# Transposed input requested from ScalarE's queue, warm-up on a cleared buffer, last square sum on VectorE

## The chip, the cores and the metric

The kernel runs on one core of a Trainium2 chip. Its time is the device time of one execution, in microseconds (us); three executions of the kernel before took 984.0, 983.96 and 982.06 us, with a median of 983.96. One more execution was recorded by the hardware profiler, and all rows below come from that one.

## The reference

Two layers of a hybrid decoder act on x, 256 positions of 2048 features. Each layer normalises x, multiplies it by one wide input matrix, feeds three causal mixers from the result (a convolution, a gated delta rule, a dilated attention), and adds the gated mixer outputs through one output matrix:

```
for l in range(2):
    h = x * rsqrt(mean(x*x) + eps) * norm_w[l]
    u = h @ w_in[l]                          # 2048 x 7692
    y = [conv(u) | gated_deltanet(u) | dilated_attention(u)], each times silu(gate)
    x = x + y @ w_out[l]                     # 2048 x 2048
out = x * rsqrt(mean(x*x) + eps) * final_norm_w
```

## The kernel before, in words

Every large product is made from three partial products: a float32 operand is split into a high part, rounded by ScalarE (`split_hi`, or the first line of `split`), and the rest, made by VectorE (`split_lo`, or its second line). TensorE adds high x high, high x low and low x high into a PSUM tile `acc`. The tiles HT_71 and HT_72 hold high and low part of the normalised input, whi and wlo those of a weight piece.

For layer 0 the input is read a second time in a layout by channel, x_t: 16 blocks of 128 channels x 256 positions. `load_xt` reads one or two blocks into a buffer b_0 to b_8 and `norm_xt` splits them with the layer's weight column from the parameter tile par; so block k of HT needs an x_t transfer, one ScalarE and one VectorE instruction. The row scale rsqrt(mean(x*x)) is applied later to the products; its square sums come from x itself, read in eight pieces by `load_x`, squared and added up on ScalarE.

Weights arrive in pieces (`load_weights`), in four raw buffers, requested by SyncE's queue (SP). A raw buffer is free again when VectorE has made its wlo. `project` walks over the jobs. The first job has 396 columns: for each of the 16 channel blocks one `unit` of six products (two row tiles, three parts each). The sixteen units take nine weight pieces: two of one block, seven of two blocks.

The order of the instructions on each engine is not that of the code. The class `Plan` runs all the generators as tasks, gives each instruction an assumed duration, and appends next the one that could start first in that reckoning. What it assumes decides the order; the engines then work through their lists strictly as written, with semaphores between them. A DMA takes one of eight semaphores in turn (DMAHW0 to DMAHW7), and a request waits at its engine until the DMA that had the same semaphore before has landed.

At the end, the last job makes its two row tiles one after the other (`last_unit`). For each, `last_residual` adds the residual, sums the squares of the last 256 columns, finishes the row scale on VectorE and GpSimd, multiplies by the final weight, scales and writes out.

Of the kernel before, what the change touches and what calls it, by code (L numbers as in the profile page):

```python
# [11 lines left out]
F32 = mybir.dt.float32  # L12
F32R = mybir.dt.float32r
BF16 = mybir.dt.bfloat16
AF = mybir.ActivationFunctionType
ALU = mybir.AluOpType
# [5 lines left out]
S = 256  # L22
DEPTH = 2
# [141 lines left out]
def _free(ap):  # L165
    n = 1
    for s in ap.shape[1:]:
        n *= s
    return n
# [3 lines left out]
def hybrid_trunk(ctx, tc, x, x_t, w_in, conf_pw_w, w_out, params, final_norm_w, rope, lnc, out):  # L173
    nc = tc.nc
    cp = ctx.enter_context(tc.tile_pool(name="consts", bufs=1))
    wp = ctx.enter_context(tc.tile_pool(name="weights", bufs=1))
    sp = ctx.enter_context(tc.tile_pool(name="work", bufs=1))
# [3 lines left out]
    plan = Plan()  # L181


    def act(out_, in_, func=AF.Copy, scale=1.0, bias=0.0, accum=None):
        n_ap = sum(not isinstance(v, (int, float)) for v in (scale, bias)) + (accum is not None)
        kw = {} if accum is None else {"accum_out": accum}
        return ("act", 95 + _free(out_) / 1.2 + 93 * n_ap,
                lambda: nc.scalar.activation(out_, in_, func, bias=bias, scale=scale, **kw))  # L188
# [6 lines left out]
    def tt(out_, a, b, op):  # L195
        return ("dve", 70 + _free(out_) / 0.96, lambda: nc.vector.tensor_tensor(out_, a, b, op=op))  # L196

    def ts(out_, a, s1, s2, op0, op1=None):
        extra = 60 if not isinstance(s1, (int, float)) else 0

        def emit():
            if op1 is None:
                nc.vector.tensor_scalar(out_, a, s1, None, op0=op0)  # L203
            else:
                nc.vector.tensor_scalar(out_, a, s1, s2, op0=op0, op1=op1)
        return ("dve", 70 + _free(out_) / 0.96 + extra, emit)
# [32 lines left out]
    def summax(out_, a, b, mx):  # L239

        return ("dve", 130 + _free(out_) / 0.96, lambda: nc.vector.tensor_tensor_reduce(
            out=out_, in0=a, in1=b, scale=1.0, scalar=-3.0e38, op0=ALU.add, op1=ALU.max, accum_out=mx))

    def gpow(out_, a, e):
        return ("pool", 350 + 165 * _free(out_), lambda: nc.gpsimd.tensor_tensor(out_, a, e, op=ALU.pow))  # L245

# [18 lines left out]
    JUNK = sp.tile([128, 512], BF16, name="JUNK")  # L265
# [7 lines left out]
    def small(shape, name):  # L273
# [4 lines left out]

    xf = x.rearrange("b s d -> (b s) d")
    of = out.rearrange("b s d -> (b s) d")  # L280
    ident = cp.tile([128, 128], F32, name="ident")
    make_identity(nc, ident)
    ones = cp.tile([128, 128], F32, name="ones")
# [6 lines left out]
    PAR = [cp.tile([128, PCOLS], F32, name=f"par{l}") for l in range(DEPTH)]  # L290
# [2 lines left out]
    PIECES, LAST_PIECES = W_OUT_BLOCKS  # L293
    GROUPS = [(0, 768), (768, 768), (1536, 512)]
    X_PIECES = [(256 * i, 256) for i in range(8)]
    XT_BEFORE = {0: (0, 1), 1: (1, 1), **{i: (2 * i - 2, 2) for i in range(2, 9)}}
    X_BEFORE = {8 + j: j for j in range(len(X_PIECES))}
    SSQ = [cp.tile([128, NT, len(p)], F32, name=f"ssq{l}")
           for l, p in enumerate([X_PIECES] + [PIECES] * (DEPTH - 1) + [LAST_PIECES])]
# [8 lines left out]
    def warm_up(n):  # L308

        ps = yield ("get", MIX)  # L310
        yield ("pe", 107.0, lambda: [nc.tensor.transpose(ps[:, :128], ones, ident) for _ in range(n)])
        yield ("put", MIX, [ps])

    def setup_consts():
# [10 lines left out]
    def setup(l):  # L325

        if l:
            yield ("wait", conv_ready[0])
        yield ("dma", 200.0 if l else 0.0, lambda: (nc.sync if l else nc.scalar).dma_start(PAR[l], params[l]))
        yield ("set", misc_ready[l])  # L330
        yield act(AEXP[l], PAR[l][:, P_AL:P_AL + H], AF.Exp)
        yield ts(PAR[l][:, P_DW:P_DW + 4 * CW], PAR[l][:, P_DW:P_DW + 4 * CW], 0.5, None, ALU.mult)
        yield ts(GNH[l], PAR[l][:, P_GN:P_GN + 1], 0.5, None, ALU.mult)
        yield ("set", conv_ready[l])

    def split(hi, lo, src, scale):

        yield act(hi, src, scale=scale)
        yield stt(lo, src, scale, hi.bitcast(F32), ALU.mult, ALU.subtract)
# [19 lines left out]
    def load_xt(k0, m):  # L359

        buf = yield ("get", S768)
        yield ("dma", 128 * m * S * 4 / 330.0, lambda: nc.sync.dma_start(  # L362
            buf[:, :m * S], bass.AP(tensor=x_t.tensor, offset=x_t.offset + k0 * S, ap=[[KB * S, 128], [1, m * S]])))
        plan.spawn(norm_xt(k0, m, buf), 2)

    def norm_xt(k0, m, buf):
        yield ("wait", misc_ready[0])
        for b in range(m):
            k = k0 + b
            yield from split(HT[0][:, k, :], HT[1][:, k, :], buf[:, b * S:(b + 1) * S], PAR[0][:, k:k + 1])  # L370
            yield ("set", h_ready[0][k])
        yield ("put", S768, [buf])

    def load_x(j):

        c0, n = X_PIECES[j]
        buf = yield ("get", S768)
        xs = buf[:, :NT * n].rearrange("p (t c) -> p t c", t=NT)
        yield ("dma", 128 * NT * n * 4 / 330.0, lambda: nc.sync.dma_start(
            xs, xf[:, c0:c0 + n].rearrange("(t p) c -> p t c", p=128)))  # L380
        plan.spawn(sums_x(j, xs, buf), 3)
        if j == len(X_PIECES) - 1:
            nc.sync.dma_start(lncs, lnc)
            nc.sync.dma_start(ropes, rope.rearrange("(t p) c -> p t c", p=128))
# [5 lines left out]
    def load_weights(order):  # L390
        for i in order:
            src, m, n, _ = chunks[i]
            if i in XT_BEFORE:
                yield from load_xt(*XT_BEFORE[i])
            if i in X_BEFORE:
                yield from load_x(X_BEFORE[i])
            raw = yield ("get", RAW)
            view = raw[:, :m * n].rearrange("p (a n) -> p a n", n=n)
            flat_ = raw[:, :m * n]
            if m > 2:  # L400
                flat_ = flat_.rearrange("p (a n) -> p a n", n=2 * n)
            raw_ready[i][1] = (raw, view)
            yield ("dma", 128 * m * n * 4 / 330.0,
                   lambda src=src, flat_=flat_: nc.sync.dma_start(flat_, src))  # L404
            yield ("set", raw_ready[i][0])
# [158 lines left out]
    def layer(l):  # L564
# [612 lines left out]
        def last_residual(j):  # L1177

            c0, n = pieces[j]
            end = j == len(pieces) - 1  # L1180

            def then(acc, tile_=None):
                yield ("wait", xs_ready[j // 2])
                if j == 0:
                    plan.spawn(load_final(), 30)
                for t in range(NT) if tile_ is None else [tile_]:
                    xv = xs[j][t]
                    yield tt(xv, acc[t][:, :n], xv, ALU.add)
                    yield act(JUNK[:, :n], xv, AF.Square, accum=SSQ[DEPTH][:, t, j:j + 1])
                    if end:  # L1190
                        plan.spawn(finish_norm(DEPTH, [], t, t + 1), 1)
                    elif j == len(pieces) - 2:
                        m = sums[:, t:t + 1]
                        yield ("dve", 90.0, lambda: nc.vector.tensor_reduce(m, SSQ[DEPTH][:, t, :j + 1], AX.X, ALU.add))
                        yield ts(m, m, 1.0 / D, 1e-6, ALU.mult, ALU.add)
                    yield ("wait", fw_ready)
                    yield tt(xv, xv, FW[j], ALU.mult)
                    if end:
                        plan.spawn(final(t), 2)
                if not end:  # L1200
                    yield ("put", ACC, [acc])
            return then

        def load_final():
            bufs = yield ("get", S768, 3)
            for j, (c0, n) in enumerate(LAST_PIECES):
                FW[j] = bufs[j // 2][:, (j % 2) * 384:(j % 2) * 384 + n]
                nc.gpsimd.dma_start(FW[j], bass.AP(tensor=final_norm_w.tensor, offset=final_norm_w.offset + c0,
                                                   ap=[[0, 128], [1, n]]))
            yield ("pool", 8000.0, lambda: None)  # L1210
            yield ("set", fw_ready)

        def final(t):
            yield ("wait", final_ready[t])
            r = RSTD[DEPTH][:, t:t + 1]
            for g, eng in ((2, "dve"), (0, "act"), (1, "dve")):
                c0, n = GROUPS[g]
                xv = xg[g][t]
                dma = nc.scalar if eng == "act" else nc.sync
                yield act(xv, xv, scale=r) if eng == "act" else ts(xv, xv, r, None, ALU.mult)  # L1220
                dma.dma_start(of[t * 128:(t + 1) * 128, c0:c0 + n], xv)
                plan.now.end = 0.0
# [31 lines left out]
        return jobs, bg  # L1254

    setup_consts()
    plan.spawn(warm_up(10), 0)
    plan.spawn(warm_up(5), 0, 5000.0)
    for l in range(DEPTH):
        plan.spawn(setup(l), 40 if l else -2)  # L1260
    plan.spawn(finish_norm(0, nsq0), 3)
# [69 lines left out]
```

## Time and profile before

| what | value |
|---|---|
| median of three runs | 983.96 us (982.06 to 984.0) |
| profiled execution | 982.4 us |
| its span, first to last instruction | 980.7 us |
| TensorE busy | 968.4 us, 99% |
| VectorE busy | 749.3 us, 76% |
| ScalarE busy | 550.8 us, 56% |

The profiled execution is 1.7 us longer than its span, and 1.56 us under the median of the runs. TensorE is busy from 12.7 us to 972.4 us almost without a gap; what is not TensorE lies in the first 13 us and the last 8 us.

### The profile page before, as it was taken

To read this page: it belongs to the slowest core of one execution; us is meant where nothing else is said; L and a number is where in the kernel's file an instruction comes from. 1 tells how busy PE (TensorE), PEld (TensorE's weight loads), DVE (VectorE), ACT (ScalarE), POOL (GpSimd) and SP (SyncE) were. 2 spreads that over 40 slices of the span, in tenths; PEclk is the share of its full clock that TensorE was granted. 3 is DMA by queue.
4 is the path that set the end of the run, shared out by engine and by line. 5 is a ranking of instruction groups with operands and counts; after the bars stand their busy time and mean duration, and the time that the engine had idled before them with its cause. 6 is when DMAs were issued, how large, how long until landed. Compare 5 with 4: busy or idle time off the path is not lost.

```text
span 980.7 us, 19060 instructions
## 1 busy us (share of the span) xinstructions
PE 968.4 (99%) x7259; PEld 946.3 (96%) x7259; DVE 749.3 (76%) x1519; ACT 550.8 (56%) x1079; POOL 48.5 (5%) x70
## 2 busy tenths in 40 slices
PE   8999999999999999999999999999999999999996
PEld 7999999999999999999899999999899999999996
DVE  7687799999999666655558768999999976666672
ACT  7764355446685764554455633554466767544551
POOL 1002100200010000000000020002000100000000
PEclk9999999999999999999999999999999999999998
DMA  9765565644445535776655545556344556366672
GB/s 328 254 195 169 175 191 180 186 146 145 146 138 174 178 113 181 224 239 219 214 190 193 192 161 175 186 180 188 128 147 140 155 182 200 127 192 213 220 248 87
DMA packets 67037, 179.01 MB, mean 183 GB/s; under 512 B 8000, under 2 KB 12224, under 8 KB 66944
## 3 DMA queue, kind: packets, MB, share of 16 engines
q1 hardware_dynamic: 64880, 173.85, 54.7%
q0 software_dynamic: 1632, 3.02, 1.2%
q8 instruction: 57, 0.93, 0.4%
q10 hardware_dynamic: 432, 0.91, 0.3%
q14 instruction: 36, 0.29, 0.1%
HBM read 172.77 MB, written 4.98 MB: 181 GB/s over the span
## 4 chain that ended last, share of the span: by engine, by line
PE 97%; DVE 1%; DMA 1%; issue 1%; SPq 0%; ACT 0%; POOLq 0%; POOL 0%; DVEq 0%; ACTq 0%
PE acc L448 87%; PE mix L229 6%; PE mix L236 3%; DMA b<-in_x_t 1%; PE acc L457 1%; PE mix L747 0%; DVE wlo L196 0%; DVE b L193 0%; SPq L404 0%; SPq L362 0%; DVE inv L209 0%; ACT whi L188 0%; POOLq L1327 0%; POOL rstd L245 0%; DVE PTs L203 0%
## 5 line engine op out<-in xcount | busy, mean ns | idle before, releaser
L188 ACT ACTIVATE whi<-raw 128x768 fp32r<-128x768 f32 (+4 forms) x389 | 339.7, 873 | 361.4 <-PE acc L448 320.6
L196 DVE TENSOR_TENSOR wlo<-raw,whi 128x768 fp32r<-128x768 f32 (+4 forms) x389 | 385.5, 991 | 186.4 <-ACT whi L188 182.7
L448 PE MATMUL acc<-HT,whi 128*128 128x256 f32 x2304 | 411.0, 280 | 0.0
L448 PEld LDWEIGHTS acc<-HT,whi 128*128 128x128 f32 x2304 | 351.6, 188 | 1.5 <-issue 1.5
L448 PE MATMUL acc<-HT,wlo 128*128 128x256 f32 x1152 | 321.4, 279 | 0.0
L448 PE MATMUL acc<-whi,HT 128*128 128x384 f32 (+1 forms) x1024 | 271.1, 346 | 0.7 <-ACT whi L188 0.6
L448 PEld LDWEIGHTS acc<-HT,wlo 128*128 128x128 f32 x1152 | 216.0, 188 | 0.0
L448 PEld LDWEIGHTS acc<-whi,HT 128*128 128x128 f32 x1024 | 180.1, 189 | 3.3 <-ACT whi L188 1.4
L448 PE MATMUL acc<-wlo,HT 128*128 128x384 f32 (+1 forms) x512 | 172.9, 338 | 0.8 <-DVE wlo L196 0.8
L448 PE MATMUL acc<-whi,YT 128*128 128x384 f32 (+2 forms) x640 | 163.0, 338 | 0.0
L193 DVE SCALAR_TENSOR_TENSOR b<-b,par,b 128x255 f32<-128x255 f32 (+20 forms) x348 | 153.6, 465 | 0.3
L448 PEld LDWEIGHTS acc<-whi,YT 128*128 128x128 f32 x640 | 114.3, 187 | 2.8
L448 PE MATMUL acc<-wlo,YT 128*128 128x384 f32 (+2 forms) x320 | 107.9, 337 | 0.0
L448 PEld LDWEIGHTS acc<-wlo,HT 128*128 128x128 f32 x512 | 96.2, 188 | 1.8 <-DVE wlo L196 1.8
L448 PEld LDWEIGHTS acc<-wlo,YT 128*128 128x128 f32 x320 | 60.1, 188 | 1.5
L188 ACT ACTIVATE b<-mix 128x384 f32<-128x384 f32 (+3 forms) x96 | 39.6, 425 | 20.1 <-PE mix L229 12.6
L229 PE MATMUL mix<-b,b 128*128 128x128 f32 (+5 forms) x456 | 46.0, 285 | 0.0
L236 PE MATMUL mix<-ident,b 128*128 128x128 f32 x280 | 45.7, 274 | 0.0
L229 PEld LDWEIGHTS mix<-b,b 128*128 128x128 f32 (+3 forms) x456 | 36.2, 161 | 6.7 <-issue 2.2
L236 PEld LDWEIGHTS mix<-ident,b 128*128 128x128 f32 x280 | 34.2, 140 | 3.7 <-issue 1.3
L193 DVE SCALAR_TENSOR_TENSOR b<-b,b 128x256 f32<-128x256 f32 (+3 forms) x62 | 31.5, 511 | 2.6 <-ACT b L188 2.5
L188 ACT ACTIVATE b<-b,stat 128x128 f32<-128x128 f32 (+1 forms) x68 | 29.1, 442 | 6.0 <-DVE stat L203 5.9
(146 smaller groups left out, 613.2 us busy)
## 6 DMA issues: line engine op xcount, KB each, us to landing
raw<-in_w_in SPq DMA_DIRECT2D x240, 384.0 KB, 3.0
raw<-in_w_in SPq DMA_DIRECT2D x48, 512.0 KB, 3.6
raw<-in_w_out SPq DMA_DIRECT2D x64, 384.0 KB, 3.6
raw<-in_w_out SPq DMA_DIRECT2D x12, 512.0 KB, 4.1
raw<-in_w_in SPq DMA_DIRECT2D x15, 396.0 KB, 3.7
b<-in_x SPq DMA_DIRECT2D x10, 256.0 KB, 5.7
raw<-in_conf_pw_w SPq DMA_DIRECT2D x4, 512.0 KB, 3.2
raw<-in_w_out SPq DMA_DIRECT2D x8, 256.0 KB, 3.5
```

Of the source, the lines that this page charges most:

```text
L188: lambda: nc.scalar.activation(out_, in_, func, bias=bias, scale=scale, **kw))
L193: lambda: nc.vector.scalar_tensor_tensor(out_, a, s, b, op0=op0, op1=op1))
L196: return ("dve", 70 + _free(out_) / 0.96, lambda: nc.vector.tensor_tensor(out_, a, b, op=op))
L229: nc.tensor.matmul(o, a, b, start=f[0], stop=f[1])
L236: nc.tensor.transpose(o, a, ident)
L448: nc.tensor.matmul(o, w, m, start=first and i == 0 and not (chan and t % 2), stop=last and i == 2, skip_group_check=chan)
L457: nc.tensor.matmul(acc[t][:, :n], YT[w][:, k, s], HT[m][:, k, :n], start=k == 0 and i == 0, stop=k == KB - 1 and i == 2)
```

## The change

The nine x_t transfers leave SP's list and are requested by ScalarE, by one task that asks for all of them at once; the planner is told that each request occupies ScalarE for 60 ns, and that their data is there at 2600 + 1100 k0 ns. The 15 warm-up transposes, which waited for GpSimd's constants, become 8 products of a buffer that VectorE clears first. The square sum of the last 256 columns becomes one VectorE instruction with an accumulator (`sumsq`) in place of a ScalarE one.

```
--- before.py
+++ after.py
@@ -241,6 +241,10 @@
         return ("dve", 130 + _free(out_) / 0.96, lambda: nc.vector.tensor_tensor_reduce(
             out=out_, in0=a, in1=b, scale=1.0, scalar=-3.0e38, op0=ALU.add, op1=ALU.max, accum_out=mx))
 
+    def sumsq(out_, a, s_):
+        return ("dve", 130 + _free(out_) / 0.96, lambda: nc.vector.tensor_tensor_reduce(
+            out=out_, in0=a, in1=a, scale=1.0, scalar=0.0, op0=ALU.mult, op1=ALU.add, accum_out=s_))
+
     def gpow(out_, a, e):
         return ("pool", 350 + 165 * _free(out_), lambda: nc.gpsimd.tensor_tensor(out_, a, e, op=ALU.pow))
 
@@ -278,6 +282,8 @@
 
     xf = x.rearrange("b s d -> (b s) d")
     of = out.rearrange("b s d -> (b s) d")
+    blank = sp.tile([128, 128], F32, name="blank")
+    nc.vector.memset(blank, 0.0)
     ident = cp.tile([128, 128], F32, name="ident")
     make_identity(nc, ident)
     ones = cp.tile([128, 128], F32, name="ones")
@@ -293,7 +299,7 @@
     PIECES, LAST_PIECES = W_OUT_BLOCKS
     GROUPS = [(0, 768), (768, 768), (1536, 512)]
     X_PIECES = [(256 * i, 256) for i in range(8)]
-    XT_BEFORE = {0: (0, 1), 1: (1, 1), **{i: (2 * i - 2, 2) for i in range(2, 9)}}
+    XT_PIECES = [(0, 1), (1, 1)] + [(2 * i, 2) for i in range(1, 8)]
     X_BEFORE = {8 + j: j for j in range(len(X_PIECES))}
     SSQ = [cp.tile([128, NT, len(p)], F32, name=f"ssq{l}")
            for l, p in enumerate([X_PIECES] + [PIECES] * (DEPTH - 1) + [LAST_PIECES])]
@@ -308,7 +314,7 @@
     def warm_up(n):
 
         ps = yield ("get", MIX)
-        yield ("pe", 107.0, lambda: [nc.tensor.transpose(ps[:, :128], ones, ident) for _ in range(n)])
+        yield ("pe", 107.0, lambda: [nc.tensor.matmul(ps[:, :128], blank, blank, start=True, stop=True) for _ in range(n)])
         yield ("put", MIX, [ps])
 
     def setup_consts():
@@ -326,7 +332,8 @@
 
         if l:
             yield ("wait", conv_ready[0])
-        yield ("dma", 200.0 if l else 0.0, lambda: (nc.sync if l else nc.scalar).dma_start(PAR[l], params[l]))
+        yield ("dma", 200.0, lambda: nc.sync.dma_start(PAR[l], params[l])) if l else (
+            "act", 60.0, lambda: nc.scalar.dma_start(PAR[l], params[l]))
         yield ("set", misc_ready[l])
         yield act(AEXP[l], PAR[l][:, P_AL:P_AL + H], AF.Exp)
         yield ts(PAR[l][:, P_DW:P_DW + 4 * CW], PAR[l][:, P_DW:P_DW + 4 * CW], 0.5, None, ALU.mult)
@@ -359,9 +366,13 @@
     def load_xt(k0, m):
 
         buf = yield ("get", S768)
-        yield ("dma", 128 * m * S * 4 / 330.0, lambda: nc.sync.dma_start(
+        yield ("act", 60.0, lambda: nc.scalar.dma_start(
             buf[:, :m * S], bass.AP(tensor=x_t.tensor, offset=x_t.offset + k0 * S, ap=[[KB * S, 128], [1, m * S]])))
-        plan.spawn(norm_xt(k0, m, buf), 2)
+        plan.spawn(norm_xt(k0, m, buf), 2, 2600.0 + 1100.0 * k0)
+
+    def load_all_xt():
+        for p in XT_PIECES:
+            yield from load_xt(*p)
 
     def norm_xt(k0, m, buf):
         yield ("wait", misc_ready[0])
@@ -390,8 +401,6 @@
     def load_weights(order):
         for i in order:
             src, m, n, _ = chunks[i]
-            if i in XT_BEFORE:
-                yield from load_xt(*XT_BEFORE[i])
             if i in X_BEFORE:
                 yield from load_x(X_BEFORE[i])
             raw = yield ("get", RAW)
@@ -1186,7 +1195,10 @@
                 for t in range(NT) if tile_ is None else [tile_]:
                     xv = xs[j][t]
                     yield tt(xv, acc[t][:, :n], xv, ALU.add)
-                    yield act(JUNK[:, :n], xv, AF.Square, accum=SSQ[DEPTH][:, t, j:j + 1])
+                    if end:
+                        yield sumsq(JUNK[:, :n], xv, SSQ[DEPTH][:, t, j:j + 1])
+                    else:
+                        yield act(JUNK[:, :n], xv, AF.Square, accum=SSQ[DEPTH][:, t, j:j + 1])
                     if end:
                         plan.spawn(finish_norm(DEPTH, [], t, t + 1), 1)
                     elif j == len(pieces) - 2:
@@ -1254,8 +1266,8 @@
         return jobs, bg
 
     setup_consts()
-    plan.spawn(warm_up(10), 0)
-    plan.spawn(warm_up(5), 0, 5000.0)
+    plan.spawn(warm_up(8), 0)
+    plan.spawn(load_all_xt(), -1)
     for l in range(DEPTH):
         plan.spawn(setup(l), 40 if l else -2)
     plan.spawn(finish_norm(0, nsq0), 3)
```

Since the planner's clocks change at the start, the order changes on all engines. The head of ScalarE's list before (DMA rows are requests; `waits` names the semaphores; par is the parameter tile, b_0 to b_8 the x_t buffers, raw and whi the weight pieces):

```order
L329 DMA par_146<-in_params 128x237
L188 ACT_TABLE_LOAD
L188 ACTIVATE aexp_150<-par_146 128x6 [waits DMAHW0_49]
L188 ACTIVATE HT_71<-b_0_85,par_146 128x256 [waits DMAHW1_49]
L188 ACTIVATE whi_79<-raw_75 128x396 [waits DMAHW2_49]
L188 ACTIVATE HT_71<-b_1_86,par_146 128x256 [waits DMAHW3_49]
```

The head of ScalarE's list now:

```order
L188 ACTIVATE aexp_152<-par_148 128x6 [waits DMAHW0_49]
L369 DMA b_1_86<-in_x_t 128x256
L369 DMA b_2_87<-in_x_t 128x512
L369 DMA b_3_88<-in_x_t 128x512 [waits DMAHW1_49]
L369 DMA b_4_89<-in_x_t 128x512 [waits DMAHW2_49]
L369 DMA b_5_90<-in_x_t 128x512 [waits DMAHW3_49]
L369 DMA b_6_91<-in_x_t 128x512 [waits DMAHW4_49]
L369 DMA b_7_92<-in_x_t 128x512 [waits DMAHW5_49]
L369 DMA b_8_93<-in_x_t 128x512 [waits DMAHW6_49]
L188 ACTIVATE HT_71<-b_0_85,par_148 128x256
L188 ACTIVATE HT_71<-b_1_86,par_148 128x256 [waits DMAHW7_49]
L188 ACTIVATE whi_79<-raw_75 128x396
```

Eight x_t requests now stand between the exponential (aexp) and the first split of an x_t block, and six of them carry waits of their own. DMAHW4, 5 and 6 were taken last by raw_77, raw_78 and par_149, which stand in SP's list now:

```order
L413 DMA raw_75<-in_w_in 128x396
L413 DMA raw_76<-in_w_in 128x396
L413 DMA raw_77<-in_w_in 128x792
L413 DMA raw_78<-in_w_in 128x792
L335 DMA par_149<-in_params 128x237
L413 DMA raw_75<-in_w_in 128x792 [waits DMAHW7_49,DMAHW1_49,DVE_49]
```

The nine x_t requests that stood among these weight requests are gone, and the parameters of layer 1 have come forward to the fifth place.

The end of VectorE's list before (acc_123 is the last row tile, ssq its square sum, rstd the row scale, b_11 the final weight):

```order
L196 TENSOR_TENSOR b_10_95<-acc_123,b_10_95 128x256 [waits PE_49]
L205 TENSOR_SCALAR rstd_157<-ssq_154,sums 128x1 [waits Activation_49]
L196 TENSOR_TENSOR b_10_95<-b_10_95,b_11_96 128x256 [waits DVE_49]
L203 TENSOR_SCALAR b_10_95<-b_10_95,rstd_157 128x512 [waits DVE_49,Pool_49]
L203 TENSOR_SCALAR b_6_91<-b_6_91,rstd_157 128x768
```

And now (b_8 is the final weight here; the two ISA rows are the square sum and the read of its accumulator):

```order
L196 TENSOR_TENSOR b_7_92<-acc_123,b_7_92 128x256 [waits PE_49]
L245 ISA JUNK,ssq_156<-b_7_92 128x256 [waits DVE_49]
L245 ISA ssq_156 128x1
L196 TENSOR_TENSOR b_7_92<-b_7_92,b_8_93 128x256 [waits DVE_49]
L205 TENSOR_SCALAR rstd_159<-ssq_156,sums 128x1
L203 TENSOR_SCALAR b_7_92<-b_7_92,rstd_159 128x512 [waits Pool_49]
L203 TENSOR_SCALAR b_9_94<-b_9_94,rstd_159 128x768
```

The instruction that writes rstd now stands behind the product with the final weight; before it stood ahead of it.

## Rows read from the trace of the kernel before

**Rows 1.** page: engine busy time and share, then the chain of waits by engine

```profile
PE 968.4 (99%) x7259; PEld 946.3 (96%) x7259; DVE 749.3 (76%) x1519; ACT 550.8 (56%) x1079; POOL 48.5 (5%) x70
...
PE 97%; DVE 1%; DMA 1%; issue 1%; SPq 0%; ACT 0%; POOLq 0%; POOL 0%; DVEq 0%; ACTq 0%
```

**Rows 2.** windows: stretch, its length, each engine's busy time, granted clock, DMA share, GB/s

```profile
1.58:4.66 3.08, 3.08 (x15) 3.06 (x15) 2.48 (x5) 1.98 (x4) 2.53 (x4) 1.00 0.85 224
4.66:7.00 2.34, 2.22 (x10) 1.69 (x8) 1.47 (x4) 1.28 (x3) 0.00 (x0) 1.00 0.97 333
7.00:10.00 3.00, 2.02 (x9) 1.16 (x8) 2.01 (x4) 1.85 (x4) 0.00 (x0) 1.00 0.96 313
...
100.00:500.00 400.00, 400.00 (x2919) 387.64 (x2918) 311.33 (x639) 224.35 (x432) 13.35 (x16) 1.00 0.56 179
```

**Rows 3.** timeline of TensorE: start, duration, engine, line, operation, count

```profile
1.58 3.46 PE L311 MATMUL mix<-ident,ones 128*128 128x128 f32 x15 [1.58 <-POOL pw_neg L316]
...
4.70 1.01 PE L448 MATMUL acc<-whi,HT 128*128 128x396 f32 x2
...
20.58 0.52 PE L448 MATMUL acc<-whi,HT 128*128 128x396 f32 x2
...
21.12 0.52 PE L448 MATMUL acc<-whi,HT 128*128 128x396 f32 x2
...
25.45 0.40 PE L448 MATMUL acc<-HT,whi 128*128 128x256 f32 x2
...
93.06 2.17 PE L229 MATMUL mix<-b 128*128 128x128 f32 x18
```

**Rows 4.** timeline of ScalarE and SP's requests, first 4 us

```profile
0.80 0.41 ACTq L329 DMA_DIRECT2D par<-in_params  x1
1.24 1.28 ACT L188 ACT_TABLE_LOAD   x1 [1.24 <-PEq L1319]
1.25 0.42 SPq L404 DMA_DIRECT2D raw<-in_w_in  x1
...
1.72 0.42 SPq L362 DMA_DIRECT2D b<-in_x_t  x1
...
3.58 0.21 ACT L188 ACTIVATE aexp<-par 128x6 f32<-128x6 f32 x1 [1.05 <-DMA par<-in_params]
...
3.69 0.49 ACT L188 ACTIVATE HT<-b,par 128x256 fp32r<-128x256 f32 x1
```

**Rows 5.** DMA issues, first 20 us: count, KB each, median us to landing

```profile
raw<-in_w_in SPq DMA_DIRECT2D x7, 396.0 KB, 5.8
```

**Rows 6.** groups by form, ScalarE, first 26 us: busy us, mean ns, idle before

```profile
L188 ACT ACTIVATE HT<-b,par 128x256 fp32r<-128x256 f32 x16 | 7.4, 497 | 1.8 <-DMA b<-in_x_t 1.8
L188 ACT ACTIVATE whi<-raw 128x792 fp32r<-128x792 f32 x7 | 6.0, 864 | 0.9 <-DVE HT L193 0.6 <-DMA raw<-in_w_in 0.4
L188 ACT ACTIVATE JUNK<-b 128x256 bf16<-128x256 f32 x8 | 3.3, 411 | 0.2
...
L188 ACT ACTIVATE whi<-raw 128x396 fp32r<-128x396 f32 x2 | 1.1, 526 | 0.3 <-DMA raw<-in_w_in 0.3
```

**Rows 7.** groups by form, VectorE, first 26 us

```profile
L196 DVE TENSOR_TENSOR wlo<-raw,whi 128x396 fp32r<-128x396 f32 x2 | 1.1, 568 | 0.4 <-ACT whi L188 0.4
```

**Rows 8.** timeline of the end, last row tile

```profile
972.42 0.42 DVE L196 TENSOR_TENSOR b<-acc,b 128x256 f32<-128x256 f32 x1 [2.66 <-PE acc L457]
972.88 0.42 ACT L188 ACTIVATE JUNK<-b 128x256 bf16<-128x256 f32 x1 [3.20 <-DVE b L196]
...
973.42 0.21 DVE L205 TENSOR_SCALAR rstd<-ssq,sums 128x1 f32<-128x1 f32 x1 [0.58 <-ACT JUNK L188]
973.55 0.42 DVE L196 TENSOR_TENSOR b<-b,b 128x256 f32<-128x256 f32 x1
```

**Rows 9.** timeline of VectorE: an accumulating instruction and its accumulator read

```profile
754.25 0.42 DVE L241 CUSTOM_DVE_ANT_0 b<-mix,lncs 128x256 f32<-128x256 f32 x1
754.59 0.08 DVE L241 DVE_READ_ACCUMULATOR2_ANT stat<- 128x1 f32 x1
```

More of the change, by code (lines that the diff above doesn't have):

```diff
@@ L242, in summax, with sumsq @@
             out=out_, in0=a, in1=b, scale=1.0, scalar=-3.0e38, op0=ALU.add, op1=ALU.max, accum_out=mx))
+    def sumsq(out_, a, s_):
+        return ("dve", 130 + _free(out_) / 0.96, lambda: nc.vector.tensor_tensor_reduce(
+            out=out_, in0=a, in1=a, scale=1.0, scalar=0.0, op0=ALU.mult, op1=ALU.add, accum_out=s_))
     def gpow(out_, a, e):
@@ L280, in hybrid_trunk @@
     of = out.rearrange("b s d -> (b s) d")
+    blank = sp.tile([128, 128], F32, name="blank")
+    nc.vector.memset(blank, 0.0)
     ident = cp.tile([128, 128], F32, name="ident")
@@ L295, in hybrid_trunk @@
     X_PIECES = [(256 * i, 256) for i in range(8)]
-    XT_BEFORE = {0: (0, 1), 1: (1, 1), **{i: (2 * i - 2, 2) for i in range(2, 9)}}
+    XT_PIECES = [(0, 1), (1, 1)] + [(2 * i, 2) for i in range(1, 8)]
     X_BEFORE = {8 + j: j for j in range(len(X_PIECES))}
@@ L310, in warm_up @@
         ps = yield ("get", MIX)
-        yield ("pe", 107.0, lambda: [nc.tensor.transpose(ps[:, :128], ones, ident) for _ in range(n)])
+        yield ("pe", 107.0, lambda: [nc.tensor.matmul(ps[:, :128], blank, blank, start=True, stop=True) for _ in range(n)])
         yield ("put", MIX, [ps])
@@ L328, in setup @@
             yield ("wait", conv_ready[0])
-        yield ("dma", 200.0 if l else 0.0, lambda: (nc.sync if l else nc.scalar).dma_start(PAR[l], params[l]))
+        yield ("dma", 200.0, lambda: nc.sync.dma_start(PAR[l], params[l])) if l else (
+            "act", 60.0, lambda: nc.scalar.dma_start(PAR[l], params[l]))
         yield ("set", misc_ready[l])
@@ L361, in load_xt, with load_all_xt @@
         buf = yield ("get", S768)
-        yield ("dma", 128 * m * S * 4 / 330.0, lambda: nc.sync.dma_start(
+        yield ("act", 60.0, lambda: nc.scalar.dma_start(
             buf[:, :m * S], bass.AP(tensor=x_t.tensor, offset=x_t.offset + k0 * S, ap=[[KB * S, 128], [1, m * S]])))
-        plan.spawn(norm_xt(k0, m, buf), 2)
+        plan.spawn(norm_xt(k0, m, buf), 2, 2600.0 + 1100.0 * k0)
+    def load_all_xt():
+        for p in XT_PIECES:
+            yield from load_xt(*p)
     def norm_xt(k0, m, buf):
@@ L392, in load_weights @@
             src, m, n, _ = chunks[i]
-            if i in XT_BEFORE:
-                yield from load_xt(*XT_BEFORE[i])
             if i in X_BEFORE:
@@ L1188, in then @@
                     yield tt(xv, acc[t][:, :n], xv, ALU.add)
-                    yield act(JUNK[:, :n], xv, AF.Square, accum=SSQ[DEPTH][:, t, j:j + 1])
+                    if end:
+                        yield sumsq(JUNK[:, :n], xv, SSQ[DEPTH][:, t, j:j + 1])
+                    else:
+                        yield act(JUNK[:, :n], xv, AF.Square, accum=SSQ[DEPTH][:, t, j:j + 1])
                     if end:
@@ L1256, in hybrid_trunk @@
     setup_consts()
-    plan.spawn(warm_up(10), 0)
-    plan.spawn(warm_up(5), 0, 5000.0)
+    plan.spawn(warm_up(8), 0)
+    plan.spawn(load_all_xt(), -1)
     for l in range(DEPTH):
```

## The prediction

> **What bounds the kernel now.** I read the page first: TensorE is busy 968.4 of 980.7 us and the chain of waits is 97% TensorE [rows 1]. The windows tell where it is not: in 100 to 500 us it is busy 400.00 of 400, but 2.02 of 3.00 us in 7 to 10 [rows 2]. So a gain or loss comes from the first 13 us, from the end, or from a stall that a new order makes in the middle. The timeline gives the size of the first: the first job begins at 4.70 us and the second at 25.45 us, 20.75 us apart [rows 3]. In the steady part three of its products take 0.54 us (20.58 to 21.12), so six take 1.085 and its sixteen units 17.4 us [rows 3]. 3.4 us are therefore waits, for x_t blocks, their splits and the weights; they are all that a better start could give back, apart from an earlier first product.
>
> **The x_t requests, which decide.** Before, ScalarE issues one request, for the parameters (0.41 us), loads its table until 2.52, waits for the parameters until 3.58, and makes the first x_t split at 3.69 [rows 4]. Now eight x_t requests stand between that exponential and the first split. A request is not free for the engine that issues it: the table load starts when the request of 0.80 + 0.41 us is over, and on SP consecutive requests are 0.47 us apart (1.25 to 1.72) [rows 4]. Eight times 0.47 after 3.58 + 0.1 (the split followed the exponential by 0.11) is 7.45 us: the first split cannot come sooner. That is the low end, 3.8 us later than before.
>
> Six of these requests also wait for a semaphore's last user. The last two wait for raw_78 and par_149, the fourth and fifth requests on SP, issued near 0.80 + 3 x 0.47 = 2.2 us and at 2.7. A weight piece of 396 KB landed 5.8 us after its request in these 20 us (median) [rows 5], so raw_78 is there at 8.0. From bytes: 224 GB/s for 3.08 us and 333 for 2.34 make 0.69 + 0.78 = 1.47 MB by 7.0 us [rows 2]; everything through par_149 is 1.59 MB, so at the 313 GB/s of the next window [rows 2] 7.4 us if x_t takes no share. If x_t takes half from 5.5 us on (0.97 MB moved by then, 0.62 left at 165 GB/s), 9.25. I take 8.4 for par_149, near the 8.0 of the nearest row. The last request goes out then, and the first split starts at 8.85 (7.9 to 9.7).
>
> TensorE's first product now stands behind two splits and a weight split: 7.4/16 = 0.46 each, and 0.53 [rows 6]. So it starts at 8.85 + 1.45 = 10.3 us, not 4.70. What is got for it: all x_t is on its way by then, and the waits for it go. Late next are ScalarE's and VectorE's splits. After the first weight piece the unit waits for its low part (0.57 [rows 7]); the third and fourth pieces (0.86 each [rows 6]) follow with x_t splits between them, so that the first four units need about 5.1 us in place of 4.34: 0.8 us. Afterwards ScalarE has, from 8.85, 16 x 0.46 + 7 x 0.86 + 2 x 0.53 + five square sums at 0.6 (0.41 [rows 6] and the read of the sum) + 0.2 = 17.7 us of work before the last block is split: 26.6, under TensorE's own end, so it does not bound, but it leaves little. A square sum that waits there for its x piece holds up the splits behind it; I take 0.3 us (0 to 1.3).
>
> **The warm-up.** The 15 transposes took 3.46 us, 0.23 each; products of the same shape took 2.17/18 = 0.12 later [rows 3]. The granted clock reads 1.00 all along [rows 2], so it is the pace that shows the lower level (1.2 GHz), and by 20.58 the upper (2.4). The 8 products take 8 x 0.23 = 1.85 us, from about 1.1 us on (VectorE's clearing comes first), in time in which TensorE has nothing else; cost 0. But then it idles from 3 to 10.3 us. If it starts at half pace for as long as it did before (1.58 to about 5.3), 1.85 us are lost; if at full pace, nothing. Part of it lies beside the waits of the first units; I take 0.7.
>
> The Trainium skill (TensorE: Matmul & The Clock Gate, What's actually happening) says that an idle TensorE falls back to 1.2 GHz. The trace agrees in the pace of the first transposes; by this rule the 0.7 would be nearer 1.2 and the total 0.5 us more.
>
> Sum for the first job: 10.3 + 17.4 + 0.8 + 0.3 + 0.7 = 29.5 us against 25.45: **+4.0 us**. Ends: 7.45 + 1.45 + 17.4 + 0.8 = 27.1 (+1.6); 9.7 + 1.45 + 17.4 + 0.8 + 1.3 + 1.85 = 32.5 (+7.0). TensorE has no slack later, so nothing of it is given back.
>
> **SP's list** loses nine requests and their waits. Its next weight requests wait for VectorE's low parts, which come later now; with four pieces in hand this costs nothing beyond the terms above.
>
> **The last square sum.** Before: VectorE's addition starts at 972.42, ScalarE's square at 972.88, rstd at 973.42, the product with the final weight at 973.55, beside GpSimd [rows 8]. Now VectorE squares at about 972.88: 0.34 us to its accumulator read and 0.08 for that (754.25 to 754.59 [rows 9]) make 973.30, 0.1 sooner. But the product with the final weight comes next in its list, and rstd behind it: 0.34 us more (the same pitch), so 973.67, **+0.25 us** (-0.1 to 0.45). The first row tile's turn lies beside the products of the second and costs nothing.
>
> **The new order elsewhere.** No row shows it. ScalarE and VectorE are busy 56% and 78% of 400 us while TensorE never waits [rows 1, 2], and the planner's rules are the same. I take 0 (-0.5 to +2).
>
> Total +4.25 us: 982.4 + 4.25 = 986.65 on the profiled execution. That lies 1.56 under the median of the runs; on the median it would be 988.2. I state the middle: **987.4 us**, from a base of 983.2. About 0.2% (2 us of 984) is what a measurement here can tell from no change.
>
> **Rivals.**
> Only the issue counts (0.13). The semaphores are free when ScalarE comes to them. For it: the parameters landed 2.8 us after their request (0.80 to 3.58) [rows 4]; against it: 5.8 us for a weight piece [rows 5]. First split 7.45, job end 27.1: +1.6 + 0.25, 985.0, no difference one can measure.
> The Trainium skill (DMA: Bandwidth & Descriptors, Issuing engines are not separate DMA queues) says that requests from a second engine save only the sequencer's time to issue them, since all use the same 16 DMA engines. That would save SP 9 x 0.47 = 4.2 us of issue and no transfer time; by this rule alone, with ScalarE paying, the sum is that of this case. No row before shows two engines asking at once beyond the one parameter request.
>
> Faster (0.04): x_t arrives early and ScalarE is not held. If requests are handed on at once and the first split comes at about 3.7 us as before, the 3.4 us of waits vanish: 983.2 - 3.4 + 0.25 = 980.0. For it: TensorE's waits in 7 to 10 us are waits for data [rows 2]. Against it: the table load began only when the request was over [rows 4]. It decides when the first product starts before 25.45 - 17.4 = 8.05 us, against the 8.9 that issue alone allows.
>
> Everything late (0.13): transfers share evenly (first split 9.7), half pace on top, a held square sum: +7.0 + 0.25, 990.5; a stall from the new order would add to it.
>
> **The numbers.** Forecast 0.70, with its own range 985.5 to 989.5; the rivals 0.13, 0.04, 0.13. The range, 984.2 to 990.8, leaves out the fast case, the lower part of the issue-only case and the tail of the late one. Slower by over 0.2%: the forecast nearly whole, the late case and a fifth of the issue-only one, 0.85; within 0.2%: 0.11; faster: 0.04.
>
> **What would show it.** In the new profile: ScalarE without work from about 3.8 to 8.9 us with the requests in it, the last at about 8.4; TensorE's first 396-column product near 10.3 and the first 256-column one near 29.5; no unit waiting for x_t after it; rstd of the last row tile 0.25 us later after TensorE's end than before. Wrong if the first split comes under 6 us, if the second job starts before 27, or if TensorE shows idle stretches after 40 us.

## The result, and the profile after

The kernel after took 988.11 us in the median of six executions (987.22 to 988.41); six of the kernel before on the same chip took 982.4 (981.76 to 984.0). The ratio is 1.0053, with a 95% interval of 1.0041 to 1.0065: slower by half a per cent. One of the twelve executions of a kernel below, with two blocks on ScalarE, took 1186.56 us at a granted clock of 0.752, and its ratio leaves that one out. The profiled execution of the kernel after took 988.18 us, of which 986.5 are its span, 5.8 more than before.

The first and fourth part of its page, busy times and the chain of waits by engine:

```profile
PE 970.6 (98%) x7260; PEld 949.9 (96%) x7260; DVE 750.2 (76%) x1521; ACT 550.2 (56%) x1078; POOL 48.2 (5%) x70
...
PE 97%; DMA 1%; DVE 1%; issue 1%; ACT 0%; POOLq 0%; ACTq 0%; POOL 0%; DVEq 0%
```

Set beside [rows 1], TensorE is busy 2.2 us longer in a span that is 5.8 us longer. So 3.6 us are idle time, and 2.2 are products that took longer. These are two different things to look for.

The timeline of ScalarE and its requests, first 10 us of the kernel after (start, duration, engine, line, operation, count; in brackets the idle time before it and what ended it):

```profile
0.80 0.41 ACTq L336 DMA_DIRECT2D par<-in_params  x1
1.25 0.45 ACTq L369 DMA_DIRECT2D b<-in_x_t  x1
1.73 1.28 ACT L188 ACT_TABLE_LOAD   x1 [1.73 <-PEq L1331]
...
3.87 5.27 ACTq L369 DMA_DIRECT2D b<-in_x_t  x8
9.19 0.91 ACT L188 ACTIVATE HT<-b,par 128x256 fp32r<-128x256 f32 x2 [5.12 <-DMA b<-in_x_t]
```

Where [rows 4] show the first split at 3.69, eight requests now hold ScalarE from 3.87 to 9.14, and the split comes at 9.19. The last two of the eight, in a narrower stretch of the same timeline:

```profile
8.33 0.82 ACTq L369 DMA_DIRECT2D b<-in_x_t  x2
```

The trace has the landings too. The last three requests go out at 7.32, 8.33 and 8.70 us, each 0.02 to 0.06 us after the landing of the transfer that had the same semaphore: raw_77 at 7.30, raw_78 at 8.31, par_149 at 8.65.

The timeline of TensorE, kernel after: warm-up, first job, and the first product of the second job:

```profile
1.12 3.48 PE L317 MATMUL mix<-blank 128*128 128x128 f32 x16 [1.12 <-DVE blank L286]
10.57 1.03 PE L457 MATMUL acc<-whi,HT 128*128 128x396 f32 x2 [5.97 <-ACT whi L188]
...
11.73 0.86 PE L457 MATMUL acc<-whi,HT 128*128 128x396 f32 x2
...
14.58 0.53 PE L457 MATMUL acc<-whi,HT 128*128 128x396 f32 x2
...
29.74 0.40 PE L457 MATMUL acc<-HT,whi 128*128 128x256 f32 x2
```

TensorE idles 5.97 us between warm-up and first product. Set beside [rows 3], the first job begins 5.87 us later and the second 4.29: the first job now has no wait, but its pairs of products (the lines with x2) take 0.86 us up to 14 us, and only then the 0.52 of [rows 3]. The windows say why (stretch, its length, each engine's busy time, granted clock, DMA share, GB/s):

```profile
5.00:7.00 2.00, 0.00 (x0) 0.00 (x0) 0.00 (x0) 0.00 (x0) 0.00 (x0) 1.00 0.98 317
7.00:10.00 3.00, 0.00 (x0) 0.00 (x0) 0.27 (x1) 0.81 (x2) 0.00 (x0) 0.60 1.05 395
10.00:13.00 3.00, 2.42 (x7) 2.32 (x8) 2.87 (x7) 3.00 (x9) 0.00 (x0) 0.50 0.96 323
...
100.00:500.00 400.00, 400.00 (x2923) 387.68 (x2922) 309.61 (x633) 222.84 (x428) 16.43 (x22) 1.00 0.57 178
```

TensorE does nothing from the end of the warm-up at 4.60 to 10.57 us. The granted clock is still 1.00 from 5 to 7 us and 0.60 in the mean of 7 to 10, so it falls while TensorE is idle; from 10 to 13 us it is 0.50 (1.2 GHz). In the kernel before it is 1.00 from 7 to 10 us [rows 2], and from 10 to 13 too. From 100 to 500 us TensorE is as full as before.

The timeline of the last row tile, kernel after:

```profile
978.47 0.42 DVE L196 TENSOR_TENSOR b<-acc,b 128x256 f32<-128x256 f32 x1 [2.57 <-PE acc L466]
978.93 0.43 DVE L245 CUSTOM_DVE_ANT_0 JUNK<-b 128x256 bf16<-128x256 f32 x1
979.28 0.08 DVE L245 DVE_READ_ACCUMULATOR2_ANT ssq<- 128x1 f32 x1
979.40 0.42 DVE L196 TENSOR_TENSOR b<-b,b 128x256 f32<-128x256 f32 x1
979.75 0.20 DVE L205 TENSOR_SCALAR rstd<-ssq,sums 128x1 f32<-128x1 f32 x1
```

From the addition to rstd it is 1.28 us, against 1.00 in [rows 8]: the product with the final weight stands between, as the order said. GpSimd is 0.11 us quicker here, so the scaling starts 2.15 us after the addition, against 2.00.

The 5.8 us of the span, as differences of these timelines: second job +4.29; second job to last job +1.76 (937.02 against 935.26 us); last addition to scaling +0.15; from the scaling to the end of the span -0.44. The second of these terms was not in the prediction, and TensorE has no wait there. It is the pace of products. The chain of waits of the kernel after has this piece (start, duration, what, count):

```profile
99.56 43.11 PE acc L457 x366
```

The same 366 products in another execution of the kernel before, which had a span of 982.7 us:

```profile
95.45 43.11 PE acc L448 x366
```

And in a third execution of the kernel before, with a span of 981.0 us:

```profile
95.56 41.49 PE acc L448 x366
```

The first profiled execution has 41.49 us too. A 256-column product takes 0.1133 us there and 0.1178 in the others. Between 60 and 700 us the first and third profile of the kernel before have 419 products at the faster pace, nearly all of them from 95 to 143 us, and the second has 4. The instructions are the same ones, so this comes and goes from one execution of the same kernel to the next. Two profiles of the kernel after (spans 986.5 and 986.1) have 3 such products each in these 640 us. Against the execution without the stretch the kernel after is 3.74 us longer in its span: +4.07 second job, -0.05 in the middle, +0.14 and -0.43 at the end. That is what the change costs between profiles without the stretch; the other 2.0 us of the comparison come with a stretch that the profile of the kernel before happened to have. A later execution of the kernel after agrees: 987.81 us, where the kernel before took 984.32 in the median of 15 on the same chip.

### The profile page after: what moved, and what is told of

Its sections match the earlier page's. It is cut to its first block, busy times and chain, and to the rows that moved or that the text cites. A ratio compares the mean times of both kernels' runs of the same rounds, so it can differ in the third digit from the quotient of the medians.

```text
span 986.5 us, 19068 instructions
## 1 busy us (share of the span) xinstructions
PE 970.6 (98%) x7260; PEld 949.9 (96%) x7260; DVE 750.2 (76%) x1521; ACT 550.2 (56%) x1078; POOL 48.2 (5%) x70
## 4 chain that ended last, share of the span: by engine, by line
PE 97%; DMA 1%; DVE 1%; issue 1%; ACT 0%; POOLq 0%; ACTq 0%; POOL 0%; DVEq 0%
PE acc L457 87%; PE mix L229 6%; PE mix L236 3%; PE acc L466 1%; DMA b<-in_x_t 0%; DMA par<-in_params 0%; PE mix L756 0%; DVE b L193 0%; DVE wlo L196 0%; DVE inv L209 0%; ACT HT L188 0%; DVE b L196 0%; POOLq L1339 0%; ACTq L369 0%; POOL rstd L249 0%
```

## The experiments

All start from the kernel after unless said otherwise. In the comparisons below the kernel before took 983.92 us (two times 17 executions, with the same median both times; 984.32 of 15 for the last comparisons). In the result's six, two were near 984 and four near 982, so that its ratio has some of that stretch in it.

**x_t back on SP.** The other two parts stay.

```
-        yield ("act", 60.0, lambda: nc.scalar.dma_start(
+        yield ("dma", 128 * m * S * 4 / 330.0, lambda: nc.sync.dma_start(
...
-    plan.spawn(load_all_xt(), -1)
```

> The change without its x_t part: the requests are back in SP's list, the warm-up of 8 products of a cleared buffer and the square sum on VectorE stay. Theory (ScalarE is held by the requests): first x_t split near 3.7 us, first 396-column product at 4.5 to 5, second job at 25.3 to 25.7, end of the last product to the last scaling 0.15 us longer than before; time within 0.2% of before. Rival (the shorter warm-up makes the products slow): second job at 26.5 or later, time 1 us or more over before.

984.14 us, ratio 1.0006 (0.9997 to 1.0015). First split at 3.66, first product at 4.63, second job at 25.04, 0.41 before that of [rows 3]. The loss is in the x_t part. Its timeline of TensorE:

```profile
4.63 0.63 PE L454 MATMUL acc<-whi,HT 128*128 128x396 f32 x2
...
25.04 0.40 PE L454 MATMUL acc<-HT,whi 128*128 128x256 f32 x2
```

Here the product comes right behind the warm-up, and its pair takes 0.63 us, not 1.03.

**The x_t part alone.** Transposes and ScalarE's square as in the kernel before.

```
-        yield ("pe", 107.0, lambda: [nc.tensor.matmul(ps[:, :128], blank, blank, start=True, stop=True) for _ in range(n)])
+        yield ("pe", 107.0, lambda: [nc.tensor.transpose(ps[:, :128], ones, ident) for _ in range(n)])
...
+                    yield act(JUNK[:, :n], xv, AF.Square, accum=SSQ[DEPTH][:, t, j:j + 1])
...
+    plan.spawn(warm_up(10), 0)
+    plan.spawn(warm_up(5), 0, 5000.0)
```

> The x_t part of the change alone, with the warm-up of 15 transposes and the square sum on ScalarE as before. Theory: first split near 9.2 us, first 396-column product near 10.5, second job near 29.7, total 4 to 6 us over before. Rival (warm-up): under 3 us over before.

987.7 us, ratio 1.0042 (1.0028 to 1.0057). Its timeline of ScalarE:

```profile
3.92 4.71 ACTq L369 DMA_DIRECT2D b<-in_x_t  x8
8.67 0.91 ACT L188 ACTIVATE HT<-b,par 128x256 fp32r<-128x256 f32 x2 [4.55 <-DMA par<-in_params]
```

The idle time before the split ends with the landing of layer 1's parameters, the semaphore that the last request waits for. Its timeline of TensorE:

```profile
10.06 1.03 PE L457 MATMUL acc<-whi,HT 128*128 128x396 f32 x2 [5.01 <-ACT whi L188]
...
11.21 0.86 PE L457 MATMUL acc<-whi,HT 128*128 128x396 f32 x2
```

The second job begins at 28.98. With transposes the first pairs after the idle time take 1.03 and 0.86 us as well: what the warm-up multiplies is not the cause.

**All requests ahead of everything.** If the requests were slow because they stand behind the exponential, moving them ahead should help.

```
+        if not l:
+            yield from load_all_xt()
...
-    plan.spawn(load_all_xt(), -1)
```

> The changed kernel with all nine x_t requests ahead of the exponential in ScalarE's list, so that they need not wait for the parameters. Theory (held engine): the last request goes out at 5.5 to 7.5 us, the first split follows it at 6 to 8, second job at 26.5 to 28.5, total 1 to 3.5 us over before. Rival (bandwidth: all the x_t data and weights are simply too much for the first 10 us): second job stays near 29.5.

990.07 us, ratio 1.0065 (1.0051 to 1.0079). It failed: the second job begins at 31.83, 2.1 us later than in the kernel after. Its timeline of ScalarE:

```profile
1.25 7.65 ACTq L371 DMA_DIRECT2D b<-in_x_t  x9
8.93 1.28 ACT L188 ACT_TABLE_LOAD   x1 [8.93 <-DMA b<-in_x_t]
...
10.34 0.89 ACT L188 ACTIVATE HT<-b,par 128x256 fp32r<-128x256 f32 x2
```

The requests begin 2.6 us sooner and end at 8.9 all the same: their end is set by landings, not by the cost of issuing. The longest hold is the seventh request's, which goes out at 7.60, when ScalarE's own second x_t block has landed (7.58); that block had been asked for at 1.73 and landed right behind a weight piece that SP asked for at 1.71 (7.30). And the table load, which had been hidden behind the parameters, now stands in the open.

**A warm-up that lasts.** 36 products in place of 8.

```
-    plan.spawn(warm_up(8), 0)
+    plan.spawn(warm_up(36), 0)
```

> The changed kernel with 36 warm-up products in place of 8, so that TensorE works until about 10.7 us. Theory (1.84 us of the first two units is half pace after the idle stretch; some 0.8 of it covers waits for low parts): the 396-column products keep 0.18 us each from the start, second job at 28.6 to 29.2 in place of 29.74, total 0.5 to 1.1 us under the changed kernel. Rival (the first units wait for ScalarE and VectorE, not for the clock): second job at 29.6 or later.

987.86 us, ratio 1.0042 (1.0028 to 1.0056). Its timeline of TensorE, first job and start of the second:

```profile
11.36 0.61 PE L457 MATMUL acc<-whi,HT 128*128 128x396 f32 x2
...
28.78 0.40 PE L457 MATMUL acc<-HT,whi 128*128 128x256 f32 x2
```

Without idle time ahead of it the first job takes 28.78 - 11.36 = 17.42 us, its bare length from [rows 3]; in the kernel after it takes 29.74 - 10.57 = 19.17. So the slow clock costs 1.75 us there. The kernel after alone says about the same: its first twelve products take 4.01 us (10.57 to 14.58), the next ones 2.17 for as many. Only 0.96 of it came out, since the long warm-up itself kept the first product waiting until 11.36.

**Only two blocks on ScalarE.** They are asked for ahead of the table load, where no semaphore is in use yet; the other seven stay on SP. rstd is put ahead of the product with the final weight.

```
+        if not l:
+            yield from load_xt(0, 1)
+            yield from load_xt(1, 1)
...
+        if m == 1:
+            yield ("act", 400.0, lambda: emit(nc.scalar))
...
+        else:
+            yield ("dma", 128 * m * S * 4 / 330.0, lambda: emit(nc.sync))
...
+                        plan.spawn(finish_norm(DEPTH, [], t, t + 1), 1).base -= 120.0
```

> Only the first two x_t blocks are requested by ScalarE, ahead of its table load and of any wait; the other seven stay between the weight requests on SP as in the kernel before. Warm-up on the cleared buffer, last square sum on VectorE with rstd made ahead of the product with the final weight. If ScalarE's held requests and the late data are the loss: first x_t split at 3.7 to 4.6 us, first 396-column product at 4.5 to 5.3, second job at 24.3 to 25.3 (before 25.45), scaling at most 1.95 us after the last addition (after 2.14, before 2.00), and a time of 983 to 985 us, 0.995 to 1.001 of the kernel before. If leaving SP's list is itself harmful whatever the number of requests: second job after 27 us and a time over 986. From the second to the last job I expect 936.8 to 937.1 us, as in every other changed kernel, unless the stretch of faster products of 95 to 143 us shows here, which takes 1.8 us off.

983.87 us, ratio 1.0002 (0.9993 to 1.0011). The time is within what was expected, the start is not: first product at 6.02, second job at 25.52. Its timeline of ScalarE, and of TensorE:

```profile
1.25 0.93 ACTq L373 DMA_DIRECT2D b<-in_x_t  x2
...
5.03 0.51 ACT L188 ACTIVATE HT<-b,par 128x256 fp32r<-128x256 f32 x1 [0.64 <-DMA b<-in_x_t]
```

```profile
6.02 1.03 PE L464 MATMUL acc<-whi,HT 128*128 128x396 f32 x2 [1.12 <-ACT whi L188]
```

Asked for at 1.25, the first block is there at 5.0; asked for by SP at 0.80 it was there before 3.7 [rows 4]. But leaving SP's list for ScalarE's costs little as long as no request waits and the requests come early: the second job begins 0.48 us later than with all of x_t on SP (25.04), and the time doesn't show it. The scaling comes 1.92 us after the addition, 0.23 sooner than in the kernel after, from rstd's place.

**Splits between the requests.** The kernel after, with the planner told what a request costs.

```
-        yield ("act", 60.0, lambda: nc.scalar.dma_start(
+        yield ("act", 450.0, lambda: nc.scalar.dma_start(
...
-    plan.spawn(load_all_xt(), -1)
+    plan.spawn(load_all_xt(), 4)
```

> The kernel after, all x_t still requested by ScalarE, but the planner is told that a request costs 450 ns, so that splits stand between the requests: the first split behind the request of the fifth transfer, the second one a request later. If the hold of ScalarE behind its requests alone makes the late start: first split at about 6 us and first product at 7 to 7.5, second job near 26.5, time 984.5 to 986. If the data itself comes late, because the second block's request goes out behind SP's first weight requests and data lands in the order of the requests: first split at about 6, but the second only at 8.5 to 9.5 when its block has landed, first product at 9.5 to 10.2, second job at 28.3 to 29.6, time 987 to 988.5, as slow as the kernel after.

987.65 us, ratio 1.0036 (1.0023 to 1.0049). Its timeline of ScalarE:

```profile
3.98 1.78 ACTq L369 DMA_DIRECT2D b<-in_x_t  x4
5.81 0.51 ACT L188 ACTIVATE HT<-b,par 128x256 fp32r<-128x256 f32 x1 [1.63 <-DMA b<-in_x_t]
...
8.08 0.51 ACT L188 ACTIVATE HT<-b,par 128x256 fp32r<-128x256 f32 x1 [1.77 <-DMA b<-in_x_t]
```

And of TensorE:

```profile
9.06 1.03 PE L457 MATMUL acc<-whi,HT 128*128 128x396 f32 x2 [4.16 <-ACT whi L188]
...
28.31 0.40 PE L457 MATMUL acc<-HT,whi 128*128 128x256 f32 x2
```

The first split comes 3.4 us sooner than in the kernel after, and then ScalarE waits for the second block, asked for at 3.98 and there at 8.06. First product 9.06, second job 28.31: 1.43 us are given back of 4.29. From the second to the last job it then takes 938.53 us, 1.5 more than in the kernel after, 0.8 of them a wait of TensorE for a row scale, so that the time hardly moves. The second of the two theories holds, with the second block some 0.4 us sooner than it said: the data itself is late.

**Requests from GpSimd.** Its queue has semaphores of its own, so ScalarE is held by nothing.

```
-        yield ("act", 60.0, lambda: nc.scalar.dma_start(
+        yield ("pool", 60.0, lambda: nc.gpsimd.dma_start(
```

> The kernel after with its x_t transfers requested by GpSimd, whose queue has semaphores of its own; they stand behind the making of its constants (about 4 us). ScalarE is then held by no request. If only ScalarE's hold counted: the first split comes when the first block has landed, at 5 to 6.5 us, and the second job at 26 to 27.5; time 984.5 to 986.5. If the place of the request among SP's weight requests counts: the blocks land behind the 1.6 MB that SP asked for before 4 us, the first split at 8 us or later, second job at 28 to 31, time 987 to 989.

987.92 us, ratio 1.0039 (1.0026 to 1.0052). Its timeline of GpSimd's requests and of ScalarE:

```profile
4.09 4.95 POOL L369 DMA_DIRECT2D b<-in_x_t  x9
...
7.89 0.91 ACT L188 ACTIVATE HT<-b,par 128x256 fp32r<-128x256 f32 x2 [3.64 <-DMA b<-in_x_t]
```

And of TensorE:

```profile
9.28 1.03 PE L457 MATMUL acc<-whi,HT 128*128 128x396 f32 x2 [4.74 <-ACT whi L188]
...
28.97 0.40 PE L457 MATMUL acc<-HT,whi 128*128 128x256 f32 x2
```

ScalarE is free and waits 3.64 us for the block. Second job at 28.97, so a late block is enough for a loss of 3.5 us. Why it is late is less clear here than in the kernel with splits between the requests: the block lands 1.1 us after the last of what SP asked for (7.87 against 6.77), there 0.35 us after it (8.06 against 7.71), so that GpSimd's way of requesting may have a part in it.

**Two blocks on ScalarE, longer warm-up.** 12 products in place of 8 in the kernel with two blocks, to close its idle 1.12 us.

> The kernel with two x_t blocks on ScalarE, with 12 warm-up products in place of 8 and nothing else changed, so that TensorE has no idle time between the warm-up and its first product. There the first product came at 6.02 us, 1.12 us after the warm-up, and ran at half pace until 10.3 us; the second job began at 25.52. If the idle time is what cost the pace: first product at 6.0 to 6.4 us, its pairs 0.5 to 0.65 us from the start in place of 1.03 and 0.86, some waits for weights of 0.5 to 1 us, second job at 24.0 to 24.8, 0.7 to 1.5 us earlier, time 982.5 to 983.3 against 983.87. If the slow pace comes whatever TensorE did before: pairs of 1.03 and 0.86 again, second job at 25.5 to 25.9, time 983.8 to 984.3. If data sets the pace of the first units anyway: pairs at full pace but the waits grow by as much, second job at 25.2 or later.

983.9 us against 983.87; against the kernel before 0.9995 (0.9986 to 1.0004). No gain. Its timeline of ScalarE, and of TensorE:

```profile
7.60 0.51 ACT L188 ACTIVATE HT<-b,par 128x256 fp32r<-128x256 f32 x1 [1.49 <-DMA b<-in_x_t]
```

```profile
6.26 1.01 PE L464 MATMUL acc<-whi,HT 128*128 128x396 f32 x2
...
7.29 0.53 PE L464 MATMUL acc<-whi,HT 128*128 128x396 f32 x2
...
8.58 0.63 PE L464 MATMUL acc<-whi,HT 128*128 128x396 f32 x2 [0.59 <-ACT whi L188]
```

The pace is up after one pair, as the first theory said, but the time is that of the third: the second block, requested at the same 1.73 us, lands at 7.57, and in the profile ahead of it at 6.06, so waits for data take the place of the slow products; the second job begins at 26.07. One profile each can't tell how much of the 0.55 us is that spread.

**The two kernels again**, unchanged, for the faster stretch:

> The kernel before once more, unchanged, one profile. In its first profile 419 products of 256 columns between 95 and 143 us run at 0.1133 us each and all others at 0.1178, which is 1.9 us; no changed kernel has shown that so far. If the stretch belongs to the kernel's order, it is there again and the profiled time is about 982.4. If it comes and goes from execution to execution, a profile without it has a span of about 982.5, 1.9 us longer, and the same second job at 25.4.

> The kernel before, unchanged, a third profile. The first had 419 faster products of 256 columns and a span of 980.7 us, the second 4 between 60 and 700 us and 982.7. If the stretch comes and goes from one execution to the next, either can come here, and the span goes with it: near 980.8 with some 400 faster products, near 982.6 with none, in between with fewer.

> The kernel after, unchanged, a second profile. The start is fixed by its lists: first x_t split at 9.0 to 9.4 us, second job at 29.5 to 30.0, and last scaling 2.14 us after the last addition. If the faster stretch can come here too, the span may be up to 1.9 us under 986.5; if the kernel's order shuts it out, it is 986.3 to 986.7 again.

Before: 984.43 us with 4 faster products and a second job at 25.67, then 982.68 us with 419 and 25.81. After: 987.81 us with 3, first split at 8.68, second job at 29.38. The stretch is not the order's: the same kernel has it or not. It is not seen in full in any changed kernel, so whether they can have it is open. But shorter stretches are there: the two kernels with two blocks on ScalarE have 52 such products at 138 to 145 us, the x_t part alone has 37 at 61 to 77, and four of the changed kernels have 95 or 96 between 951 and 967, worth 0.4 us. A stretch of 70 near 840 us is in all thirteen profiles.

No version beat the kernel before by more than the measurement can tell.

## Why the prediction was right

**The requests hold ScalarE.** As it said: the first split was put at 8.85 and came at 9.19 (8.68 in the second profile), the last request at 8.4 and went out at 8.70 (8.19), right behind the landing of the parameters that it had to wait for. The requests that come before any landing cost about what was assumed. The rival in which only issue counts fails by the trace (5.27 us for eight requests, not 3.8) and by the kernel with all requests ahead, where the end of the requests did not move with their start.

**But a second cause lies right under it.** The prediction said that a held ScalarE makes the late start. Freed of it, two kernels are still 2.9 and 3.5 us late, for the second block or all of them are asked for behind SP's weights and land behind them. The prediction had no term for that landing. Holding ScalarE is worth at most 1.43 of the 4.29 us, by the kernel with splits between the requests, and more likely some 0.5: in that profile the second block also landed 0.96 us sooner, and counted from its landing the first product came after 1.00 us, against 1.55 in the kernel after. The x_t part alone, which holds ScalarE, and the kernel with GpSimd's requests, which does not, begin their second jobs at the same time (28.98 and 28.97). The rest is when the data comes: asked for at 1.73, in the kernel with two blocks on ScalarE, the second block landed at 6.06 and the second job began at 25.52. The sum was right because both end within 0.2 us of each other: in the kernel after the second block landed at 9.02, and the last request was over at 9.14. Both follow the landing of the same parameters at 8.65, which is why one term could stand for the two; that the prediction needed only one was luck. The Trainium skill (DMA: Bandwidth & Descriptors, Issuing engines are not separate DMA queues) says that a second issuing engine brings no second set of DMA engines. The trace agrees as far as it can show this: from ScalarE's queue and from GpSimd's alike, the blocks came behind what SP had asked for sooner (8.06 and 7.87 us, asked for at 3.98 and 4.09).

**First product 10.3, second job 29.5**: 10.57 and 29.74. Behind the right sum two terms were wrong and made up for each other, which was luck. The 0.7 for half pace should have been 1.75, its upper bound of 1.85 nearly; the 0.8 for waits on low parts and the 0.3 for a held square sum are not there, since the first job takes its bare 17.42 us when the clock is up. (That job starts 0.8 us later, which may hide some.) The sentence on the Trainium skill's rule (TensorE: Matmul & The Clock Gate, What's actually happening), by which idle time brings the clock back to 1.2 GHz, gave 1.2 for this term; the trace agrees with the rule, with the granted clock falling in idle time (1.00 from 5 to 7 us, 0.60 from 7 to 10) and 0.50 from 10 to 13 us, and the measured cost is higher still.

**The waits for x_t go**: no unit of the first job waits after the first. But not all of the 3.4 us were waits, and not all waits were for x_t: in the profile before, the first three products take 1.07 us (4.70 to 5.77) where later ones take 0.54, and ScalarE waited there 0.7 us for weight pieces beside the 1.8 for x_t [rows 6].

**The tail, +0.25**: +0.15. rstd is 0.28 later, of which GpSimd gave 0.11 back: its instruction takes 0.55 to 0.56 us in the seven profiles in which VectorE has already made the product with the final weight, and 0.67 in the six in which VectorE makes it beside it. Behind the scaling the span got 0.43 shorter; this goes with x_t leaving SP altogether (5.84 to 5.91 us in all kernels that do, 6.27 to 6.30 in those that don't, whatever the square sum) and was not foreseen.

**The new order elsewhere, 0**: right, -0.05 against the execution that has no faster stretch. The forecast's base, midway between the profiled execution and the median, was in effect midway between the two paces, without knowing of them. Between profiles without the stretch the change costs 3.74 us, so that the forecast's 4.25 was 0.5 too much, while its base was 1.2 under the 984.43 of that execution. That these two partly cancel, to 987.4 against 988.11, is luck too.

## What to carry to other kernels

A request is an instruction of the engine that issues it: where it must wait for a semaphore whose last user is a large transfer of another queue, everything behind it waits for that transfer. Ask also where a request comes in the order of all queues' requests: moving a small, urgent transfer to a free queue gained nothing here when it was asked for after another queue's large ones. And where TensorE's start is late, add the products that it then runs at the lower clock (here 1.75 us on 5.9 us of delay).

## What the runs showed of the hardware

- Two paces at a granted clock of 1.00: 256-column products every 0.1133 or 0.1178 us. The fast stretch of 95 to 143 us is in two of three profiles of one kernel and is worth 1.9 us; shorter ones come and go elsewhere. What sets it is open.
- The granted clock falls to 0.50 while TensorE does nothing (0.60 in the mean of 7 to 10 us, kernel after). But a reading of 1.00 near the start does not show the upper level: in the x_t part alone it reads 1.00 from 10 to 13 us, while pairs take 1.03 and 0.86 us as they do at 0.50 in the kernel after.
- The same request in the same list landed at 6.06 and at 7.57 us in two profiles of nearly the same kernel; in five other profiles the second block, asked for at 3.87 to 3.98, landed between 8.06 and 9.02, in each case 0.34 to 0.38 us after the last transfer that SP had asked for before it.
- The 8 warm-up products stand as 16 records in the trace, 0.22 us each (3.48 / 16): the prediction reckoned 8 x 0.23 = 1.85 us from the transposes, which stand once each. A product of two float32 tiles took twice that. It cost nothing, as TensorE idled after it.
